# A hybrid RWKV-7 layer on one core: the scheduler's model of time exchanged

## The chip, the cores and the metric

The kernel runs on one core of a Trainium2 chip. The time is the device time of one execution in microseconds (us). The engines are named as in the profile: PE (TensorE, matrix products), DVE (VectorE), ACT (ScalarE), POOL (GpSimd) and SP (SyncE, which here issues most of the transfers). Each engine works through its own list of instructions in order, and an instruction waits at the head of the list until the semaphores it needs have been set by other engines or by transfers. What stands on which place of these lists is decided when the kernel is built.

## The reference

One step of one layer for 128 context tokens and 512 latent tokens, 2048 wide, all in fp32:

```
h = rmsnorm(x) * (1 + sc1) + sh1                 # sh1, sc1, ... from silu(c) @ w_mod
p = h @ w_in                                     # 2048 x 5408
o_a = rwkv7(shift(p[:, :3360]))                  # 16 heads of 64, forward and backward scan
o_b = gmlp(gelu(p[:, 3360:]))                    # 8 groups of 128, chunks of 128 tokens
x = x + g1 * (concat(o_a, o_b) @ w_out)
h = rmsnorm(x) * (1 + sc2) + sh2
x = x + g2 * ((silu(h @ w_gate) * (h @ w_up)) @ w_down)
y = final_rmsnorm(x);  also the final scan states
```

The scan of each head is S = S * w_t + (S a_t) b_t^T + v_t k_t^T, y_t = S r_t. The kernel works it in chunks of 64 tokens: inside a chunk with matrices, and from chunk to chunk with a recurrence.

## The kernel before

Every wide product is three matmuls: weights and activations are split into a high and a low part (`hi`, `lo`), and hi·hi, hi·lo and lo·hi are added up. A weight piece of 256 KB arrives in `raw`; `split` (L152) makes `hi` on ACT (L160) and `lo` on DVE (L161); there are three buffers of each. With two halves of 320 tokens, a piece is used in 24 matmuls of 128x320, called wide matmuls here.

The stages, in order of time:

1. The first stage (to about 135 us): transposes of x, the modulation columns of `w_mod` (`quarter`, loads `wt` L304, 1 MB each, five buffers), the norm, the first three column blocks of `w_in`, and 20 small loads of parameter rows (`rowA`, `rowB`, L265 to L278).
2. The mixer (to about 1190 us): 43 column blocks of `w_in`, 4128 wide matmuls (`win`, L182 to L184). Four pieces make one block in PSUM (`pb`, three buffers of a half each); `take` copies it with ACT into one of three `praw` buffers (L924) and hands it to a side step. Side steps are generators in three lists (mixA, mixS, mixM), run for a budget between the wide matmuls. For each pair of heads and each direction, `take_k` has PE products `pmm` (L491) and `pwa` (L568), then ACT (L548, L571, L584, L585) and DVE (L546 to L618) build `R` and `X`, PE makes `pG` (L629), DVE `GR` and `GA` (L637, L638), PE `pXT` and `pW` (L645, L654), and the result goes to `d_S` in DRAM. `solve` and `merge` invert the 64x64 chunk matrices (`psp`, `pblk`, `pM`). `mod_all` makes further modulation columns (`pm`, L872).
3. The recurrence (to about 1520 us): for each of 8 pairs 10 chunk records `rec` of 576 KB are loaded from `d_S`. `recur` makes `w_ps` (PE L1134), adds to it (DVE L1139), makes `u_ps` (PE L1149), copies it (DVE L1152, ACT L1153), makes `s_ps` (PE L1170) and the new state `SN` (DVE L1176), which the next `w_ps` needs. Latent and context chains run side by side, and pairs start OFF = 13 hops apart. Outputs are `y_ps` (L1100, L1105), then `pO` (L1217) and `pG` (L1235). Between them stand the wide matmuls of `wout_b` (L1002 to L1004, 768 of them), the half of the output projection that does not need the recurrence.
4. The rest of the output projection (L1392 to L1394) and the feed-forward part (L1539 to L1541), to the end.

The program text gives a first order and thereby a priority:

```
        if q == 0:
            halves = [pb.tile([P, HALF], F32, tag="big", name="big") for _ in range(2)]
        win(halves, q, *parts.pop(n), step=between)
        if q == 3:
            take(b, halves)
...
        mixA.finish(b - RAW)
        pr = bp.tile([P, T], F32, tag="praw", name="praw", bufs=RAW)
        for hf in range(2):
            S.copy(pr[:, HALF * hf:HALF * hf + HALF], halves[hf])
```

The order on the engines is then worked out by the scheduler of the tile framework. It goes through the program in a model of time of its own and puts next on an engine, of the instructions that the model says are ready, the one that stands first in the text. Two models can be chosen: a default one, which the kernel before uses, and one that plays the instructions on a timeline of the engines.

## Time and profile before

| | us |
|---|---|
| median of three runs | 3417.72 (3411.99 to 3417.9) |
| profiled execution, its own time | 3414.96 |
| its span | 3413.2 |
| PE busy in the span | 3189.6 (93%) |
| granted PE clock, mean | 0.975 |

A row by stage gives for each engine the busy time and in brackets the number of instructions recorded, then the granted PE clock as a share of full speed, the busy share of the transfer engines, and GB/s. A matmul's recorded time reaches from its issue to its modelled end, and matmuls overlap; the distance between starts tells what one costs. Rows of groups end with the idle time of the engine just before them and what ended it. Four instructions of a small 64-wide group appear as eight records.

### The profile page before, as it was taken

The page shows a single profiled execution, that of the slowest core. Times are in us where ns is not written, and L with a number is a line of the kernel's source. Part 1 is how long each engine was busy: PE and PEld are TensorE (multiplying, and loading weights), DVE is VectorE, ACT ScalarE, POOL GpSimd, SP SyncE. Part 2 cuts the span into 40 slices and gives each one's busy share as a digit, 9 for nine tenths or more (in the row PEclk, how much of TensorE's full clock was granted, in tenths as well). Part 3 has the DMA queues.
Part 4 walks back from the last instruction along what each step waited for, and adds up shares of the span by engine and source line. Part 5 has one row for each costly group of instructions (what it writes and reads, how often), then busy time and mean ns, then how long its engine had stood idle before and what let it go on. Part 6 is the DMA issues. An engine that isn't in the chain of part 4 may idle for free.

```text
span 3413.2 us, 72346 instructions
## 1 busy us (share of the span) xinstructions
PE 3189.6 (93%) x28100; PEld 2905.1 (85%) x28100; DVE 2512.9 (74%) x4357; ACT 1451.5 (43%) x3172; POOL 1251.9 (37%) x1090
## 2 busy tenths in 40 slices
PE   6899989889988899989999999999999999999996
PEld 3688768768766877778999999999999999999986
DVE  4548577676766656656888888888878877877787
ACT  3334444444443433324644444444444444443365
POOL 0001121122112112321056565565666645555543
PEclk8999999999999899989999999999999999999998
DMA  8766676676767577735533434334343354543453
GB/s 322 242 191 200 194 195 175 168 204 180 198 185 193 149 221 238 219 112 158 171 113 115 125 105 126 120 110 124 112 123 113 116 178 141 153 148 114 146 165 115
DMA packets 719137, 552.94 MB, mean 162 GB/s; under 512 B 99449, under 2 KB 652425, under 8 KB 709961
## 3 DMA queue, kind: packets, MB, share of 16 engines
q1 hardware_dynamic: 706472, 534.61, 52.4%
q0 software_dynamic: 9984, 13.13, 2.0%
q8 instruction: 221, 3.62, 0.4%
q14 instruction: 124, 1.01, 0.1%
q10 hardware_dynamic: 2336, 0.57, 0.1%
HBM read 438.77 MB, written 111.69 MB: 161 GB/s over the span
## 4 chain that ended last, share of the span: by engine, by line
PE 50%; DVE 6%; issue 5%; DMA 3%; POOL 1%; ACT 1%; DVEq 0%; SPq 0%; ACTq 0%; POOLq 0%
PE P L1541 13%; PE P L1539 13%; PE P L1540 13%; DVE lo L1358 2%; PE big L1002 2%; DMA d_os<-act 1%; PE big L1003 1%; PE big L1004 1%; PE u_ps L1149 1%; PE y_ps L1105 1%; PE s_ps L1170 1%; PE pO L1217 1%; DVE act L1660 1%; PE big L1394 1%; PE big L1392 1%
## 5 line engine op out<-in xcount | busy, mean ns | idle before, releaser
L1541 PE MATMUL P<-xo,lo 128*128 128x320 f32 x2352 | 731.6, 311 | 11.1 <-DVE lo L1358 11.1
L1539 PE MATMUL P<-xo,hi 128*128 128x320 f32 x2352 | 728.2, 310 | 2.0 <-ACT hi L1357 2.0
L1540 PE MATMUL P<-xo,hi 128*128 128x320 f32 x2352 | 727.6, 309 | 0.0
L1358 DVE TENSOR_TENSOR lo<-raw,hi 128x512 fp32r<-128x512 f32 x532 | 585.9, 1120 | 64.1 <-ACT hi L1357 60.0
L1357 ACT CAST hi<-raw 128x512 fp32r<-128x512 f32 x532 | 326.4, 621 | 415.2 <-PE P L1540 320.4
L182 PE MATMUL big<-h_hi,hi 128*128 128x320 f32 x1376 | 452.1, 329 | 10.2 <-ACT h_hi L344 3.7
L1541 PEld LDWEIGHTS P<-xo,lo 128*128 128x128 f32 x2352 | 442.4, 188 | 18.9 <-DVE lo L1358 18.8
L1539 PEld LDWEIGHTS P<-xo,hi 128*128 128x128 f32 x2352 | 442.6, 188 | 2.9 <-ACT hi L1357 2.7
L1540 PEld LDWEIGHTS P<-xo,hi 128*128 128x128 f32 x2352 | 442.4, 188 | 0.0
L184 PE MATMUL big<-h_hi,lo 128*128 128x320 f32 x1376 | 436.6, 318 | 5.6 <-DVE lo L161 5.5
L183 PE MATMUL big<-h_lo,hi 128*128 128x320 f32 x1376 | 437.5, 318 | 0.5 <-DVE h_lo L345 0.5
L1452 POOL TENSOR_TENSOR raw<-raw 128x512 f32<-128x512 f32 x252 | 408.0, 1628 | 11.6 <-DVE lo L1358 1.6
L1541 PE MATMUL P<-xd,lo 128*128 128x320 f32 x1232 | 385.1, 313 | 17.8 <-DVE lo L1358 17.5
L1539 PE MATMUL P<-xd,hi 128*128 128x320 f32 x1232 | 383.7, 311 | 9.9 <-ACT hi L1357 6.8
L1540 PE MATMUL P<-xd,hi 128*128 128x320 f32 x1232 | 381.9, 310 | 0.0
L182 PEld LDWEIGHTS big<-h_hi,hi 128*128 128x128 f32 x1376 | 265.1, 193 | 76.8 <-issue 44.5
L161 DVE TENSOR_TENSOR lo<-raw,hi 128x512 fp32r<-128x512 f32 x268 | 185.7, 696 | 182.0 <-ACT hi L160 179.9
L160 ACT CAST hi<-raw 128x512 fp32r<-128x512 f32 x268 | 165.0, 618 | 295.1 <-PE big L183 122.2
L184 PEld LDWEIGHTS big<-h_hi,lo 128*128 128x128 f32 x1376 | 265.6, 193 | 12.7 <-DVE lo L161 7.4
L183 PEld LDWEIGHTS big<-h_lo,hi 128*128 128x128 f32 x1376 | 265.9, 193 | 7.9 <-issue 3.7
L1357 ACT CAST hi<-rawd 128x512 fp32r<-128x512 f32 (+1 forms) x288 | 168.7, 587 | 240.3 <-PE P L1540 222.6
L1452 POOL TENSOR_TENSOR t<-raw 128x512 f32<-128x512 f32 x84 | 135.8, 1617 | 343.1 <-DMA raw<-in_w_ffn_up_dram 325.7
(372 smaller groups left out, 6404.3 us busy)
## 6 DMA issues: line engine op xcount, KB each, us to landing
wt<-in_w_mod_dram SPq DMA_DIRECT2D x96, 1024.0 KB
raw<-in_w_ffn_gate_dram SPq DMA_DIRECT2D x182, 256.0 KB
raw<-in_w_ffn_up_dram SPq DMA_DIRECT2D x182, 256.0 KB
rec<-d_S SPq DMA_DIRECT2D x80, 576.0 KB
raw<-in_w_in_dram SPq DMA_DIRECT2D x172, 256.0 KB
rawd<-in_w_ffn_down_dram SPq DMA_DIRECT2D x128, 256.0 KB
raw<-in_w_out_dram SPq DMA_DIRECT2D x96, 256.0 KB
xd<-d_os SPq DMA_DIRECT2D x66, 320.0 KB
```

Of the source, the lines that this page charges most:

```text
L160: S.copy(hi, raw)
L161: V.tensor_sub(lo, raw, hi.bitcast(F32))
L182: TE.matmul(halves[hf], hi[:, k, :], h_hi[:, kb, s], start=(kb == 0), stop=False)
L183: TE.matmul(halves[hf], hi[:, k, :], h_lo[:, kb, s], start=False, stop=False)
L184: TE.matmul(halves[hf], lo[:, k, :], h_hi[:, kb, s], start=False, stop=(kb == KB - 1))
L1002: TE.matmul(halves[hf], hi[:, k, :], o_hi[kb][:, s], start=(k == 0), stop=False)
L1357: S.copy(hi[:, 0:nk], raw[:, 0:nk])
L1358: V.tensor_sub(lo[:, 0:nk], raw[:, 0:nk], hi[:, 0:nk].bitcast(F32))
L1452: G.tensor_tensor(out=o[:, 0:nk], in0=p[:, 0:nk], in1=q[:, 0:nk], op=ALU.subtract)
L1539: TE.matmul(ps, hi[:, k, :], xk[:, 0, :], start=f, stop=False)
L1540: TE.matmul(ps, hi[:, k, :], xk[:, 1, :], start=False, stop=False)
L1541: TE.matmul(ps, lo[:, k, :], xk[:, 0, :], start=False, stop=l)
```

## The change

The scheduler works out the order with its timeline model in place of the default one. Nothing else is touched: the same instructions on each engine, the same tiles and buffers.

```
-    with _tile.TileContext(nc) as tc:
+    with _tile.TileContext(nc, schedule_with_timeline_sim=True) as tc:
```

The order moves on all engines from the start to the end of the recurrence; behind it only a few rows differ. Wide matmuls of the mixer are counted from 1 to 4128 below, so that places in the two orders can be compared.

On PE in the mixer, behind wide matmul 2304 of before, the last `pwa` of a direction of one pair reads:

```order
L568 MATMUL pwa<-waM,wh 128x320
L568 MATMUL pwa<-waM,wl 128x320
L872 MATMUL pm_6537<-wt,cT 2x512 x3
L182 MATMUL big<-h_hi,hi 128x320
L183 MATMUL big<-h_lo,hi 128x320
L184 MATMUL big<-h_hi,lo 128x320
```

From here 132 wide matmuls follow before the `pG` (L629) of that direction. In the new order, behind wide matmul 2436, the same `pwa` reads:

```order
L568 MATMUL pwa<-waM,wh 128x320
L568 MATMUL pwa<-waM,wl 128x320
L872 MATMUL pm_6537<-wt,cT 2x512 x12
L514 MATMUL pvt<-ident,zv 128x128 x3
L629 MATMUL pG<-R,X 128x128 x8
L514 MATMUL pvt<-ident,zv 128x128 x2
L182 MATMUL big<-h_hi,hi 128x320
```

The `pG` now stands behind its `pwa` with no wide matmul between; `pm` and `pvt` are side work of other lists. Over the 16 directions the distance from the last `pwa` to the first `pG` is 26 to 132 wide matmuls before, and 0 to 101 now, with 0 three times.

On PE late in the recurrence, in the hops of the last pairs, the order of before reads as follows (`w_ps`, `y_ps` and `s_ps` belong to the chains; `gh`, `g2h` and the like to the gate of a finished pair):

```order
L1235 MATMUL pG_18343<-gq,g2h 128x320
L1002 MATMUL big<-oh,hi 128x320
L1003 MATMUL big<-ol,hi 128x320
L1004 MATMUL big<-oh,lo 128x320
L1170 MATMUL s_ps<-rec 64x64 x4
L1002 MATMUL big<-oh,hi 128x320
L1235 MATMUL pG_18349<-gh,g2h 128x320
```

And the new one, behind the gate of a pair there:

```order
L1235 MATMUL pG_17160<-gq,g2h 128x320
L1170 MATMUL s_ps<-rec 64x64 x4
L1149 MATMUL u_ps<-W,rec 64x64 x4
L1100 MATMUL y_ps<-SN,rec 64x64 x2
L1105 MATMUL y_ps<-rec 64x64 x2
```

The wide matmuls of `wout_b` are gone from between the steps. Counted by `w_ps` groups, of which there are 288, the last of the 768 stands behind group 280 before and behind group 172 now.

On SP in the first stage the transfers before are

```order
L213 DMA xall<-in_x_sample_dram 128x2048 x2
L304 DMA wt<-in_w_mod_dram 128x4x512 x11
L159 DMA raw<-in_w_in_dram 128x4x128
L304 DMA wt<-in_w_mod_dram 128x4x512
L159 DMA raw<-in_w_in_dram 128x4x128
L304 DMA wt<-in_w_mod_dram 128x4x512 x3
L159 DMA raw<-in_w_in_dram 128x4x128
L304 DMA wt<-in_w_mod_dram 128x4x512
L265 DMA rowA<-in_mu_shift_dram 24x128
L267 DMA rowA<-in_mu_shift_dram 2x128
```

and now

```order
L213 DMA xall<-in_x_sample_dram 128x2048 x2
L304 DMA wt<-in_w_mod_dram 128x4x512 x5
L159 DMA raw<-in_w_in_dram 128x4x128 x3
L265 DMA rowA<-in_mu_shift_dram 24x128
L267 DMA rowA<-in_mu_shift_dram 2x128
L269 DMA rowA<-in_mu_shift_dram 1x32
```

The 20 small row loads, which end here with `rowB`, stand behind the fifth weight load `wt` now and behind the sixteenth before; the loads of `wt` from the sixth on follow them.

## The prediction

> **What bounds the kernel now.** I read the totals first, then the busy time by stage, then TensorE's (PE's) waits, then the durations in the stages whose order moves.
>
> ```profile
> span 3413.2 us, 72346 instructions
> PE 3189.6 (93%) x28100; PEld 2905.1 (85%) x28100; DVE 2512.9 (74%) x4357; ACT 1451.5 (43%) x3172; POOL 1251.9 (37%) x1090
> ```
> ```profile
> core 0: us, PE busy (x) PEld busy (x) DVE busy (x) ACT busy (x) POOL busy (x), PEclk, DMA share, GB/s
> 200.00:1200.00 1000.00, 905.33 (x10457) 761.34 (x10457) 696.39 (x1401) 433.40 (x929) 193.47 (x306) 0.97 0.68 186
> 1200.00:1500.00 300.00, 297.84 (x4438) 236.71 (x4436) 200.73 (x660) 106.35 (x488) 74.60 (x98) 1.00 0.72 212
> 1560.00:3300.00 1740.00, 1693.45 (x11316) 1670.38 (x11315) 1409.03 (x1886) 763.17 (x1430) 929.38 (x630) 0.99 0.44 132
> ```
>
> PE sets the time nearly everywhere, so a new order pays only by what PE waits less, or by what its own instructions cost less. The mixer (200 to 1200) holds 1000 - 905.33 = 94.7 us of PE idle time, the recurrence (1200 to 1500) 2.2 us. From the rest of the output projection on PE's order stays as it was but for a few rows, so the 1740 us of the third line carry no term. The waits of the mixer:
>
> ```profile
> engine line waited for: us in total, times, longest us
> PE pG L629 <- DVE X L618: 11.5, 10, 4.0
> PE pG L629 <- DVE GA L638: 10.8, 18, 1.9
> PE psp L740 <- DVE vt L727: 8.8, 4, 3.2
> PE pwa L568 <- DVE wl L533: 7.1, 2, 3.7
> ```
>
> They are many and small: a side step's matmul reaches PE's head a little before VectorE (DVE) or ScalarE (ACT) has its operand. That is what another order can remove, and what it can make worse.
>
> **The mixer.** I followed the dependences of both orders, with durations from the trace. Three things move.
>
> First, leads. In the new order side work mostly stands further behind its source: side matmuls with less than 24 wide matmuls (one weight piece, some 3.5 us) between source and use fall from 60 of 359 groups to 15 of 337. Of the 95 us, 6 lie in dense bursts; of the other 89 I take half away, -45. The ends: 0, if PE just meets other late work, and -80, if all but the 15 short leads' share is gone. Half is nearest to the list above: a wait names only the last of several late operands.
>
> Second, dense places. At six places of the new order (wide matmuls 1668, 1860, 2436, 2628, 3684 and 3780) a chain that runs PE, ACT, DVE, PE several times stands with no wide matmul in it. The next wide matmul needs its PSUM buffer copied to `praw` by ACT (L924), and that copy stands behind the chain on ACT. What such a chain costs, from its rows:
>
> ```profile
> L548 ACT ACT_TABLE_LOAD x8 | 10.3, 1283 | 0.1
> L548 ACT ACTIVATE ssq<-ssq 128x640 f32<-128x640 f32 x8 | 5.9, 740 | 6.0 <-DVE ssq L546 5.9
> L552 DVE RECIPROCAL ssq<-ssq 128x320 f32<-128x320 f32 x16 | 34.0, 2137 | 2.2 <-ACT ssq L548 2.2
> L581 DVE TENSOR_TENSOR_SCAN L<-scan,sg 128x320 f32<-128x320 bf16 x32 | 25.4, 825 | 0.2
> L614 DVE TENSOR_TENSOR X<-tha,L 64x640 f32<-64x640 f32 x16 | 12.9, 807 | 0.0
> L618 DVE TENSOR_TENSOR X<-fs,L 64x640 f32<-64x640 f32 x8 | 6.6, 821 | 0.1
> ```
>
> At 2436, `pmm` (L491) is followed by 1.28 + 0.74 us on ACT, two reciprocals (4.3 us), two scans (1.65), and on DVE nine more passes over 640 columns at about 0.81 (7.3) before `X` (L618) is there for `pG` (L629); with what else DVE's order puts between, 27.5 us from the last wide matmul to the next. PE has 9.1 us of work in it, so 18.4 us are idle. Done alike, the six give 7.5, 8.5, 9.7, 18.2, 18.4 and 26.3: 88.6 us, against 5.8 us in all such bursts of before: +83. Three of the chains also wait for a transfer, of which the trace has this time to landing:
>
> ```profile
> d_S<-TF POOLq DMA_DIRECT2D x16, 320.0 KB, 5.6
> ```
>
> I count 4 us for each such wait, an estimate, since part of the 5.6 lies under other steps; without any of it the six come to some 65 us, with 5.6 and some lateness of the queues to 110. I take the sum, as all its other steps are rows. Before shows the small form of the same wait, where `pG` stands only 26 wide matmuls behind `pwa`:
>
> ```profile
> 1064.81 2.08 PE L629 MATMUL pG<-R,X 64*128 64x128 f32 x16 [4.03 <-DVE X L618]
> ```
> ```profile
> 1064.00:1068.00 4.00, 3.19 (x24) 1.89 (x24) 3.69 (x6) 0.91 (x2) 0.00 (x0) 0.60 0.98 262
> ```
>
> 26 at 0.15 us are 4 us of cover, and 4 us of wait are left; with 0 in their place some 8 are left for this one piece of chain.
>
> Third, changes of the PE tile's shape. A small group between wide matmuls is dear:
>
> ```profile
> 1250.95 0.31 PE L1003 MATMUL big<-ol,hi 128*128 128x320 f32 x1
> 1251.10 0.31 PE L1004 MATMUL big<-oh,lo 128*128 128x320 f32 x1
> 1251.34 0.45 PE L1149 MATMUL u_ps<-W,rec 64*64 64x64 f32 x8
> 1251.72 0.42 PE L1002 MATMUL big<-oh,hi 128*128 128x320 f32 x1
> 1251.97 0.31 PE L1003 MATMUL big<-ol,hi 128*128 128x320 f32 x1
> ```
>
> Wide matmuls start 0.15 us apart, the small group 0.24 after the last of them, the next wide one 0.38 after that, its successor 0.25. Without a change I put the group at 0.23, so the pair of changes costs 0.09 + 0.15 + 0.10 = 0.34, 0.17 each. The Trainium skill (TensorEngine Tiling (Array Packing), Key Properties) says that changing the tiling mode drains TensorE; these rows agree, and it gives no figure. The mixer's changes go from 475 to 427: -8 us. Ends 0 and -8.
>
> The weight loads on SP and the steps of POOL move with the work that uses them. I cost both at nothing: three `raw` buffers hold two pieces ahead (7 us) at a transfer share of 0.68, and POOL is busy 193.47 of 1000 us. Should a load come late, its hi cast (L160) and the wide matmuls behind it wait, which the ends of the dense places take in.
>
> Mixer: -45 + 83 - 8 = +30.
>
> **The recurrence.** Its hops are chains of small matmuls and DVE additions, and the other half of the output projection (`wout_b`, 768 wide matmuls) stands between them as cover.
>
> ```profile
> L1139 DVE TENSOR_TENSOR W<-w_ps,rec 64x128 f32<-64x128 f32 x144 | 41.5, 288 | 17.7 <-PE w_ps L1134 13.5 <-PE swap L1074 0.3
> L1152 DVE COPY rec<-u_ps 64x128 f32<-64x128 f32 x79 | 22.2, 280 | 22.3 <-PE u_ps L1149 19.1 <-PE w_ps L1134 1.8
> L1176 DVE SCALAR_TENSOR_TENSOR SN<-s_ps,gend,SG 128x64 f32<-128x64 f32 x128 | 29.7, 278 | 23.3 <-PE s_ps L1170 22.6
> ```
>
> Before, the cover lasts to `w` group 280 of 288. In the new order it is used up at 172: the last 40% of the hops stand bare, and an early stretch too. A bare hop pays w, 0.29, u, 0.28, s, two times 0.28, with only the other chain's matmuls in between. Longest chain less PE work, over all stretches without cover: 5.3 us before, 36.7 after: +31. Its lower end is 20, if the handing over from engine to engine, which my sum counts at 0.04 to 0.08 us each, hides behind the other chain; its upper end is 50, if DVE, at 200.73 of 300 busy, is late with what stands ahead of these steps in its queue. I take the sum of rows. Shape changes fall from 536 to 432: 104 x 0.17 = -18, between -10 and -18. Recurrence: +13.
>
> **The first stage.** SP (the DMA queue's engine) issues 20 small row loads between the weight loads:
>
> ```profile
> 31.28 6.87 SPq L304 DMA_DIRECT2D wt<-in_w_mod_dram  x6
> 56.87 1.16 SPq L265 DMA_DIRECT2D rowA<-in_mu_shift_dram  x1
> 71.80 1.50 SPq L304 DMA_DIRECT2D wt<-in_w_mod_dram  x3
> ```
> ```profile
> 50.00:60.00 10.00, 8.44 (x38) 4.83 (x39) 5.42 (x12) 3.17 (x5) 0.00 (x0) 0.61 1.06 375
> 60.00:70.00 10.00, 10.00 (x76) 6.55 (x74) 1.22 (x4) 0.62 (x1) 0.00 (x0) 1.00 0.61 208
> 70.00:80.00 10.00, 4.99 (x32) 2.46 (x32) 7.44 (x19) 3.48 (x5) 0.00 (x0) 0.75 0.74 257
> ```
>
> While they are issued, 56.87 to 71.80, the transfer rate falls from 375 to 208 and 257 GB/s: 2.85 MB, or 7.6 us at 375, are not moved. In the new order they stand behind the first five `wt` and three `raw`, where SP waits for a free `wt` buffer until 31 us anyway. The cover is that wait; if it is too short (14.9 us of issuing), the sixth `wt` is late by a few us. -5, between -8 and +3.
>
> **The clock.** Long waits cost twice:
>
> ```profile
> L1217 PE MATMUL pO<-I,Y 64*64 64x64 f32 x40 | 4.9, 318 | 5.5 <-POOL Y L1209 4.8 <-DVE bv L1221 0.6
> L1217 PE MATMUL pO<-J,Y 64*64 64x64 f32 x40 | 4.6, 312 | 3.3 <-POOL Y L1209 3.3
> ```
> ```profile
> 1516.00:1520.00 4.00, 3.72 (x45) 3.60 (x46) 1.51 (x3) 0.00 (x0) 0.00 (x0) 0.50 0.00 0
> 1520.00:1524.00 4.00, 2.72 (x9) 1.92 (x8) 1.09 (x2) 0.00 (x0) 0.00 (x0) 0.50 0.00 0
> 1524.00:1528.00 4.00, 4.00 (x16) 4.00 (x16) 0.41 (x1) 0.62 (x1) 0.00 (x0) 0.50 0.47 153
> ```
>
> After 8 us of waits, 12 us ran at half clock: up to 6 us lost; after the 4.03 us at 1064.81 the clock was 0.60 over 4 us, 1.6 us lost. The six long stretches so lose 10 to 36. Against that stand the mixer's 0.97, or 30 us off the full clock, which shrink with the small waits. I take +20 - 15 = +5, ends -15 and +30. The Trainium skill (TensorE: Matmul & The Clock Gate, Part 1) puts the array at half rate after an idle window of about 3.4 us until a busy one has passed; the pieces above agree, and by it alone six stretches would cost six times 1.7, an estimate of 10 us.
>
> **The sum.** -5 + 30 + 13 + 5 = +43 on the profiled execution's 3414.96 us (span 3413.2): 3458. That execution lies 2.8 us under the median, inside the runs' 3411.99 to 3417.9. A measurement tells 0.2%, 7 us, from no change.
>
> **Rivals.**
> - *The leads win (faster).* One mechanism, in the mixer: with DVE and ACT further ahead nearly all of the 89 us go (-79 in place of -45), and with these waits the half-clock pieces (-15 in place of +5). That is 54 us less than my sum: 3404. The list of small waits speaks for it; against it, a dense place starts every queue anew, and each of its steps is a measured duration. It ends under 3408 once waits and clock together give 50 us more than I put. Chance 0.15.
> - *The bare hops are slow (much slower).* The last stretch has 68 us of PE work in small groups and 30 us of idle time; if the clock falls there as it did after 1516, these groups take 318 in place of 228 ns, 1.39 times: +27, and with the upper ends of the chains (+19) and of the clock in the mixer (+10) 3514. No row of before shows the clock under such short gaps. Chance 0.22.
> - *The order does not matter.* If engines take up what they missed within a few steps, gains and losses cancel, within 7 us of 3415. The 26-matmul row speaks against it. Chance 0.05.
> - *My sum*, 3425 to 3490: 0.58.
>
> The range 3395 to 3520 leaves out under 2 in 10. Faster 0.16, same 0.05, slower 0.79; the two tails of my own case go to their neighbours.
>
> **What would show it.** Right: six PE waits of 7 to 26 us in the mixer, named by DVE `X`, ACT `praw` or `pG`; the sum of the other waits about halved; PE under 85% busy in the last 100 us of the recurrence, with waits on L1139, L1152 and L1176; GB/s without the dip at 60 to 80. Wrong: wide matmuls running on at those six places because ACT's copy comes early, or PE's idle time in the recurrence still near 2 us.

## The result and the profile after

| | before | changed |
|---|---|---|
| median of the runs | 3414.85 (3405.62 to 3417.9) | 3493.94 (3484.51 to 3500.46) |
| profiled execution, its span | 3413.2 | 3498.7 |
| granted PE clock, mean | 0.975 | 0.947 |

The changed kernel takes 1.0234 times as long (95% interval 1.0202 to 1.0266): 79 us more between the medians, 85.5 between the two profiled executions, of which the changed one is the slowest of its four. What follows is told against the profiled pair.

The head of the page of the changed kernel:

```profile
span 3498.7 us, 72391 instructions
PE 3209.6 (92%) x28100; PEld 2939.7 (84%) x28100; DVE 2502.0 (72%) x4357; ACT 1454.0 (42%) x3172; POOL 1264.5 (36%) x1090
```

Busy time does not tell it: PE has 20 us more, in 85 us more of span. The stages do. I cut both executions at the same events: the last `pm` of the first stage, the last wide matmul of the mixer, the first of `wout_b`, the last `w_ps`, the first and the last matmul of the feed-forward part. The mixer and the recurrence between such cuts, first before, then changed (stretch; its length; busy time of PE, weight loads, DVE, ACT, POOL; granted clock; transfer share; GB/s):

```profile
127.20:1163.30 1036.10, 943.71 (x10639) 793.07 (x10638) 710.01 (x1450) 448.40 (x957) 193.38 (x307) 0.97 0.67 184
1170.50:1499.10 328.60, 323.50 (x4605) 260.90 (x4605) 222.21 (x701) 118.32 (x512) 76.78 (x100) 0.99 0.72 215
```
```profile
123.50:1211.60 1088.10, 952.42 (x10518) 808.70 (x10518) 717.83 (x1445) 446.48 (x956) 198.73 (x304) 0.91 0.64 175
1213.80:1580.20 366.40, 339.74 (x4696) 289.04 (x4698) 231.31 (x717) 122.11 (x518) 80.30 (x102) 0.90 0.63 193
```

| stage | before | changed | difference | PE idle before, changed | at half clock before, changed |
|---|---|---|---|---|---|
| first stage | 127.2 | 123.5 | -3.7 | | 34.1, 30.7 |
| mixer | 1036.1 | 1088.1 | +52.0 | 92.4, 135.7 | 58.0, 198.0 |
| to the first of `wout_b` | 7.2 | 2.2 | -5.0 | | |
| recurrence | 328.6 | 366.4 | +37.8 | 5.1, 26.7 | 6.9, 71.7 |
| rest of the output projection, second norm | 227.9 | 237.8 | +9.9 | | 30.7, 37.5 |
| feed-forward part | 1659.3 | 1651.7 | -7.6 | | 13.7, 6.8 |
| tail | 26.9 | 29.0 | +2.1 | | |

So the mixer and the recurrence carry the loss, and both lose in two ways: PE idles 43 and 22 us longer, and it runs 140 and 65 us longer at half clock. PE's waits in the mixer, longest sums first:

```profile
engine line waited for: us in total, times, longest us
PE pm L872 <- DMA wt<-in_w_mod_dram: 37.2, 15, 5.2
PE pW L654 <- ACT XT L647: 21.2, 7, 6.2
PE pG L629 <- DVE X L615: 19.2, 5, 11.9
PE pG L629 <- DVE GA L638: 9.9, 8, 2.7
```

Before, the longest sum was 11.5 us and the longest wait 4.3. Now fewer waits are longer, and the first of them is `pm` for its weights, which the prediction put at nothing: its three transfers were those through `d_S`. The six dense places are where PE's long gaps lie. Their stretches from the last wide matmul to the next:

```profile
435.60:469.60 34.00, 17.09 (x91) 6.43 (x90) 21.91 (x44) 12.42 (x26) 0.74 (x1) 0.65 0.66 209
509.10:535.20 26.10, 15.98 (x280) 9.44 (x278) 20.62 (x41) 10.06 (x24) 4.33 (x9) 0.71 0.70 218
679.50:707.70 28.20, 14.45 (x70) 5.47 (x69) 23.73 (x49) 10.49 (x21) 1.23 (x1) 0.62 0.58 183
750.60:776.30 25.70, 18.23 (x317) 11.42 (x315) 19.54 (x41) 10.84 (x25) 5.61 (x9) 0.66 0.55 163
1045.90:1061.90 16.00, 7.10 (x33) 2.90 (x32) 12.65 (x24) 7.37 (x14) 3.80 (x1) 0.70 0.52 183
1085.30:1131.90 46.60, 23.53 (x363) 17.94 (x362) 26.21 (x52) 17.46 (x41) 16.48 (x28) 0.57 0.41 98
```

Length less PE busy gives 16.9, 10.1, 13.8, 7.5, 8.9 and 23.1: 80.2 us idle in 176.6 us, at a clock of 0.57 to 0.71. By name, 33.2 us of them are waits of `pm` for its weights, 17.5 waits of `pG` for `X`, 9.1 of `pwa` for `sg`; the rest is spread. In the last place, the longest, there is no wait of `pm`, and `pG` waits 11.9 us for `X`.

In the recurrence `wout_b` ends at 1471.5, and the last `w_ps` stands at 1580.2. Of that bare stretch:

```profile
1472.00:1500.00 28.00, 24.20 (x506) 20.10 (x507) 19.48 (x71) 10.20 (x56) 7.55 (x13) 0.93 0.82 254
1500.00:1540.00 40.00, 32.13 (x584) 26.02 (x582) 24.28 (x81) 12.99 (x64) 14.15 (x17) 0.76 0.72 218
1540.00:1560.00 20.00, 20.00 (x298) 16.84 (x298) 9.16 (x34) 5.33 (x36) 0.00 (x0) 0.50 0.43 129
1560.00:1580.00 20.00, 16.09 (x255) 13.25 (x254) 10.79 (x33) 6.35 (x28) 10.58 (x14) 0.81 0.20 61
```

But for one of 3.8 us for `oh` (L1392, at 1535) the waits in it are at most 1.3 us, and from 1540 to 1560 there is none at all: PE is busy for all of the 20 us, at half clock. The clock falls to half at 1496.1, for 10.2 us, at 1526.8, for 34.1, and once more at 1567.8, for 6.8. The 3.4 us just before the first two falls are

```profile
1492.70:1496.11 3.41, 1.74 (x44) 1.37 (x44) 1.46 (x5) 2.37 (x11) 3.01 (x7) 1.00 0.95 314
1523.42:1526.83 3.41, 1.81 (x42) 1.48 (x42) 2.21 (x8) 2.29 (x9) 3.24 (x6) 1.00 0.86 240
```

In both PE is busy for only half of the time, by many gaps of which none is longer than 1.3 us.

### The profile page after: what moved, and what is told of

Same layout as the page of the kernel before. It is cut to its first block, busy times and chain, and to the rows that moved or that the text cites. A ratio compares the mean times of both kernels' runs of the same rounds, so it can differ in the third digit from the quotient of the medians.

```text
span 3498.7 us, 72391 instructions
## 1 busy us (share of the span) xinstructions
PE 3209.6 (92%) x28100; PEld 2939.7 (84%) x28100; DVE 2502.0 (72%) x4357; ACT 1454.0 (42%) x3172; POOL 1264.5 (36%) x1090
## 4 chain that ended last, share of the span: by engine, by line
PE 52%; DVE 10%; DMA 7%; issue 4%; ACT 2%; POOL 1%; SPq 0%; DVEq 0%; ACTq 0%; POOLq 0%
PE P L1541 12%; PE P L1539 12%; PE P L1540 12%; DVE lo L1358 3%; DMA d_os<-act 2%; PE big L182 1%; PE big L184 1%; PE big L183 1%; PE big L1392 1%; PE big L1002 1%; PE big L1393 1%; PE big L1394 1%; DVE act L1660 1%; PE big L1004 1%; PE big L1003 1%
## 5 line engine op out<-in xcount | busy, mean ns | idle before, releaser
L182 PE MATMUL big<-h_hi,hi 128*128 128x320 f32 x1376 | 444.5, 323 | 5.1 <-ACT h_hi L344 3.2
```

The source lines that it names most:

```text
L182: TE.matmul(halves[hf], hi[:, k, :], h_hi[:, kb, s], start=(kb == 0), stop=False)
```

## The experiments

The instructions have the same names whichever model orders them. So a kernel can be built twice: once with the default model, to read the order, and then with the timeline model, with the order of chosen instructions pinned. A pin is an edge that fixes the order on one engine and adds no wait:

```
def _pin(tc, want, skip=()):
...
    info = mybir.DependencyInfo(mybir.DependencyClass.NoSync, mybir.DependencyReason.DATA)
    by = {i.name: i for i in tc.nc.cur_bb.bb.instructions}
    for names in want.values():
        for a, b in zip(names, names[1:]):
            tc.add_manual_dep(by[b], a, info, reason="pin")
...
    _, order = build(False)
    nc, order = build(True, order)
```

`_wanted(k, engine)` says which instructions are pinned; k is the place in the program text, `MARK["mix"]` the start of the mixer's code, `MARK["rec"]` that of the recurrence, `MARK["out"]` that of the part behind it. `want` holds one list for each engine. The edits below start from `return True`, which pins everything. Each run is compared with before on its own chip.

**One stage alone.** First the new order up to the end of the mixer, then the new order in the recurrence.

```
-        return True
+        return k >= MARK["rec"]
```

> The new order from the start to the end of the mixer, the order of before from the recurrence on (pinned on every engine). Theory A (the loss comes from two places that add up: mixer with its six dense places, recurrence without cover): the mixer's +48 us to its last wide matmul stay, the recurrence is as before, so 3415 + 45 = 3460 (3450 to 3470), with some 135 us of PE idle time and some 200 us at half clock up to the last wide matmul. Theory B (what is lost later is a follow-up of the mixer's delays, by the clock and by buffers that come late): the recurrence is slow again although its order is the old one, 3480 or more.

```
-        return True
+        return k < MARK["rec"] or k >= MARK["out"]
```

> The order of before up to the end of the mixer, the new one in the recurrence. Theory A: the recurrence loses what it lost in the changed kernel, 38 us from the first wide matmul of the output projection to the last w, so 3415 + 40 = 3455 (3445 to 3465); no cover behind w group 172 or so, and more than 50 us at half clock in the last 110 us of it. Theory B: 3425 or less.

The first took 3471.83 us, 1.0161 of before (1.0136 to 1.0186); the second 3439.91, 1.0069 (1.0043 to 1.0096). The two excesses add up to 2.30%, beside 2.34% for the whole change, so there are two places that add up, as theory A says. But the shares are not those I gave, 45 and 40 us; they are some 54 and 22, and both times lie outside theory A's ranges, the first by 2 us and the second by 5. The recurrences of the two runs, in this order:

```profile
1218.30:1559.20 340.90, 326.30 (x4657) 263.51 (x4653) 229.07 (x713) 120.42 (x514) 77.82 (x102) 0.98 0.69 207
```
```profile
1168.90:1517.80 348.90, 323.08 (x4618) 274.42 (x4622) 224.94 (x707) 116.81 (x506) 80.18 (x100) 0.94 0.66 202
```

A new order in the recurrence alone costs it 348.9 - 328.6 = 20 us, not 38. It is not the changed kernel's order place by place, since the model makes it anew behind the old mixer, but it has the same feature: `wout_b` ends behind `w_ps` group 176, where the changed kernel has 172, and 98 us of hops stand bare, where that has 109. PE idles as long, 25.8 beside 26.7 us; at half clock it runs for 44.4 beside 71.7. And behind the new mixer the old order costs 12 us more than before, so part of theory B holds as well. Most of those 12 is one wait:

```profile
PE pxT L1260 <- DMA x1T<-in_x_prompt_dram: 7.7, 1, 7.7
```

A load that the mixer's order leaves late on its queue is waited for at the start of the recurrence.

**The first stage alone.**

```
-        return True
+        return k >= MARK["mix"]
```

> Only the first stage in the new order, all behind it as before. The 20 small row loads stand where SP waits for a weight buffer anyway: 3 to 4 us less, 3411, with no dip of the GB/s at 60 to 80 us. Rival: the loads of the first stage are bound by the transfers in sum, and the place of the small ones is all one: 3415 within 2.

3409.26 us, 0.9983 of before (0.9964 to 1.0002). The interval just reaches 1, so the run settles nothing between the two expectations. The transfers ran without the dip:

```profile
60.00:70.00 10.00, 10.00 (x60) 7.36 (x56) 1.35 (x3) 1.21 (x2) 0.00 (x0) 0.76 1.05 386
70.00:80.00 10.00, 10.00 (x76) 6.29 (x72) 1.61 (x6) 1.82 (x3) 0.00 (x0) 1.00 1.06 378
```

But the last `pm` of the first stage stood at 126.9 us, hardly sooner than the 127.2 of before. Of the ten executions of this study with the new order in this stage, the changed kernel among them, six have it at 123.3 to 123.8 and four at 126.9 to 127.1; four more with the old order have it at 125.1 to 128.2. The four late ones share a pattern: at half clock they have 6.8 us from 58 us on, 3.4 from 89 and 3.4 from 113, where the changed kernel has 3.4 from 59 and 3.4 from 83. So the transfers lose their dip as was forecast, and in some executions the time saved is gone again, and these have more half clock. That the half clock takes it back is not shown.

**Half of the engines.** In the mixer PE in the order of before and the others free, and the reverse.

```
-        return True
+        return k >= MARK["rec"] or k >= MARK["mix"] and "PE" in str(engine)
```

> PE in the order of before from the mixer on, and all engines in the order of before from the recurrence on; in the mixer DVE, ACT, POOL and SP in the order the timeline model gives beside that. Theory A (it is PE's place for the side matmuls that makes the dense places and the small waits): PE's idle time in the mixer is near that of before, 92 us, and the time 3415 within 10. Theory B (the orders of DVE and ACT carry it, the copies to praw above all): 3440 or more, or 3400 or less if their order is what shortens the small waits.

```
-        return True
+        return k >= MARK["rec"] or k >= MARK["mix"] and "PE" not in str(engine)
```

> The counterpart of the run with PE's old order: in the mixer DVE, ACT, POOL and SP in the order of before, PE as the timeline model orders it beside them; from the recurrence on all as before. Theory A (orders fit as a set; either half alone loses): 3440 to 3480. Theory B (the order of DVE is the bad part, PE's follows it): 3415 within 10, with PE idle time in the mixer under 105 us.

Both lose far more than the whole new order of the mixer did (1.0161): 3502.99 us (1.0255, 1.0219 to 1.029) and 3531.28 (1.0348, 1.0317 to 1.038). The idle time of PE in the mixer is 1122.3 - 968.9 = 153 and 1144.0 - 974.9 = 169 us, beside 92 before and 136 changed. PE's waits in the mixer, of the first kernel and of the second:

```profile
PE pG L629 <- DVE X L615: 26.6, 8, 5.9
PE pvt L514 <- DVE zv L454: 26.1, 4, 10.9
PE pG L629 <- DVE GA L638: 14.6, 14, 3.0
```
```profile
PE pm L872 <- DMA wt<-in_w_mod_dram: 60.0, 23, 6.3
PE big L182 <- ACT hi L160: 18.8, 16, 4.9
PE big L184 <- DVE lo L161: 17.4, 15, 2.5
```

With PE as before, the other engines' free order brings `X` and `zv` late; with the others as before, PE's free order waits for weights and for the hi and lo casts. My theory A of the first run (PE's order decides) fell, and the time is in the range of theory B (3440 or more). In the second run theory B (DVE's order is the bad part) fell, and theory A (either half alone loses) holds, with a loss far above the one I gave. That an order is good only for the other engines' orders is the reading I prefer, but it is not shown: the free engines did not get the changed kernel's order, the model made a third one beside the pins. These runs also fit a model that orders badly whatever it is left to order.

**What sets the length of a dense place.** The wait that is named most there is `pm` for `wt`, and 61 `pm` matmuls, four for each weight load, stand in these places. So I kept `pm` at its old place among the wide matmuls: `KEPT` holds the `pm` and the first and third matmul of `win`, and only these are pinned.

```
-                    TE.matmul(pm[32 * j:32 * j + 2, :], ...)
+                    KEPT.add(TE.matmul(pm[32 * j:32 * j + 2, :], ...).ins.name)
...
-                    if n in at and _wanted(at[n], e):
+                    if n in at and n in KEPT:
```

> The changed kernel (3494 us) with one thing held back: the pm matmuls (L872) and the wide matmuls stand to each other on PE as before, so that the dense places hold at most 4 pm matmuls each; everything else is scheduled with the timeline model. Theory A (the chain through ACT and DVE sets how long a dense place lasts, and the waits of pm for their weights lie beside it): 3485 to 3505, more than 115 us of PE idle time in the mixer. Theory B (pm waits for its 1 MB weight load, for which there is one buffer in the mixer, and this sets the length of the places): the 37 us of such waits go, with some clock: 3440 to 3470, idle time in the mixer under 105.

3543.27 us, 1.0387 (1.0357 to 1.0417): slower than the changed kernel by 49 us, with 1140.8 - 968.3 = 172 us of idle time.

```profile
PE pvt L514 <- DVE zv L454: 31.9, 4, 12.0
PE pG L629 <- DVE X L615: 28.5, 4, 11.0
PE pW L654 <- ACT XT L647: 25.3, 12, 5.5
PE pm L872 <- DMA wt<-in_w_mod_dram: 19.2, 10, 4.1
```

The waits of `pm` halve and those for `zv`, `X` and `XT` grow by more. Theory B fell: taking the waiting `pm` away shortens nothing, and the dependent chain shows itself in its place. The time is above theory A's range, too. That the chain alone sets the length is not shown by this, since the rest of the order moved too.

**Another buffer for the blocks.** The dense places seem to lie where the wide matmuls have run ahead by all three `praw` buffers: with a fourth, they move on by one block in the order. It needs 2.5 KB, which I took from XT and GR; the control has these with one buffer, too, and three `praw`.

```
-                    GR = bk.tile([P, 4, CH], F32, tag="GR", name="GR", bufs=2)
+                    GR = bk.tile([P, 4, CH], F32, tag="GR", name="GR", bufs=1)
...
-                XT = bz.tile([P, 4, P], F32, tag="XT", name="XT", bufs=2)
+                XT = bz.tile([P, 4, P], F32, tag="XT", name="XT", bufs=1)
```

> Control for the next run: the timeline model with one buffer each for XT and GR (L636, L646, and the weights of L527 that share GR), in place of two, which frees 3 KB per partition. Five dense places in the order, most of them where the changed kernel has them (1668, 1860, 2436, 3684, 3780). Both theories: somewhat slower than the changed kernel, 3495 to 3530, for waits on the writes of XT and GR.

```
-RAW = 3
+RAW = 4
```

> As the control, with the room given to a fourth praw buffer (RAW = 4). The dense places move by one block of 96 wide matmuls (1860 to 1956, 3684 to 3780, 3780 to 3876). Theory A (a dense place is where the wide matmuls have used up the praw buffers and must wait for a side chain; one buffer more gives one block more before that): the places move but do not end, and only those are lighter that another buffer carries to the next chain: 10 to 40 us under the control. Theory B (praw has nothing to do with it): within 8 us of the control.

> The same buffers (RAW = 4, one XT, one GR) with the default model. If the mixer is limited by praw in the default order too, 10 to 20 us under before: 3395 to 3405; if the one buffer for XT and GR costs more than praw gives: 3420 to 3440.

The control took 3593.84 us (1.0528, 1.0502 to 1.0555), with a fourth buffer 3623.58 (1.0599, 1.0581 to 1.0618), and the default model with a fourth buffer 3490.02 (1.0218, 1.02 to 1.0236). All three expectations missed. The mixer, and the rest up to the last `w_ps`, of the control and of the kernel with four buffers (the second stretch starts here at the last wide matmul of the mixer):

```profile
127.10:1326.40 1199.30, 980.74 (x10518) 826.93 (x10518) 717.01 (x1444) 447.66 (x955) 198.88 (x306) 0.87 0.57 159
1326.40:1688.40 362.00, 335.42 (x4822) 285.04 (x4822) 234.27 (x722) 124.11 (x522) 82.48 (x103) 0.92 0.64 196
```
```profile
127.00:1315.30 1188.30, 970.52 (x10158) 819.45 (x10158) 710.29 (x1428) 441.99 (x944) 195.31 (x303) 0.87 0.58 159
1315.30:1698.10 382.80, 344.99 (x5180) 294.10 (x5182) 240.26 (x738) 128.59 (x534) 82.13 (x105) 0.90 0.62 190
```

PE's idle time in the mixer is 218.6 and 217.8 us: a fourth `praw` buffer takes none of it away. It lets 360 more of PE's matmuls slip behind the last wide one, and the recurrence pays for them. So the number of `praw` buffers says where a dense place lies in the order, and not what it costs. The second buffer of XT and GR, which nobody had in view, is worth some 100 us under the timeline model. It is not this model's alone: with one buffer of each, and the fourth `praw` buffer, the default model loses 74 us against before.

**The clock in the bare stretch.** In the changed kernel's own order I put 8 idle products ahead of each group of `y_ps` of the last three pairs, into columns of PSUM that nobody reads; the tile of `y_ps` is made wider for them.

```
...
+                for _ in range(FILL if p >= 5 else 0):
+                    FILLS.add(TE.matmul(yf[0][:, 128:384], gh[:, 0:P], gh[:, 0:256], start=True, stop=True).ins.name)
```

> The changed kernel in its own order (3494 us), with 8 idle products of 128x256 into unused columns of PSUM ahead of each group of y matmuls of the last three pairs: 192 matmuls, some 23 us of PE work whose result nobody reads. Theory A (in the bare stretch the clock falls because PE is not busy enough, and that costs more than the idle time): half clock in the recurrence falls from 66 us to under 35, and the time is 3475 to 3495 in spite of the added work. Theory B (the bare hops are bound by the chain alone, the clock adds little): the work fills some of the 22 us of idle time and the rest comes on top, 3500 to 3517.

3508.2 us, 1.0285 (1.0253 to 1.0316). The recurrence:

```profile
1217.50:1592.70 375.20, 358.18 (x4871) 305.93 (x4874) 231.64 (x717) 122.17 (x517) 81.42 (x103) 0.94 0.62 189
```

Its time at half clock fell from 71.7 us (the 66 of the expectation takes the clock's record 11 us too late) to 44.4, its idle time from 26.7 to 17.0, and it took 9 us longer for 23 us of products and their 48 changes of tile shape (5 to 8 us at the prices below). The clock's part shows in the time of a matmul of the same kind from 1472 to 1595, first in the changed kernel, then with the filling:

```profile
L1149 PE MATMUL u_ps<-W,rec 64*64 64x64 f32 x240 | 19.3, 267 | 3.2 <-DVE W L1139 2.9
```
```profile
L1152 PE MATMUL u_ps<-W,rec 64*64 64x64 f32 x248 | 16.5, 234 | 0.2
```

234 ns is near the 227 of before, and nearly all of the wait is gone. So that the clock falls for want of work on PE holds; that it costs more than such filling does not. The time is in theory B's range (3500 to 3517), and theory A's is missed. But B's ground, that the clock adds little, does not fit the 27 us of half clock that went, and A's mark of under 35 us was not reached either.

**The price of a change of tile shape.** The kernel before with its default model, but `wout_b` gives way after 12 wide matmuls.

```
-                yield 0.4
+                if k % 4 == 3:
+                    yield 0.4 * 4
```

> The kernel before with its default schedule, but wout_b gives way after 12 wide matmuls in place of 3, which lowers the changes of tile shape in the recurrence by some 180. At 0.17 us each (the price both traces give) that is -31 us: 3385. Rival: groups of 1.8 us are more than a hop needs and leave others bare, waits on L1139, L1152 and L1176 come up and eat half or all of it: 3400 to 3425.

3409.71 us, 0.9992 (0.9975 to 1.001): no difference that can be told. In the recurrence there is one:

```profile
1177.80:1496.20 318.40, 313.44 (x4617) 265.41 (x4618) 218.54 (x701) 119.21 (x513) 78.38 (x100) 0.99 0.73 221
```

It is 328.6 - 318.4 = 10.2 us shorter, all of it PE busy time, and no wait came up. So the time lies in the rival's range, but not by the rival's waits. The mixer, in the same order as before, took 6.8 us longer in this execution, with 20 us more at half clock. I had miscounted the changes: those between wide and small fall from 403 to 237, but groups of 64*64 and 128*64 now meet each other, and these rise from 126 to 203. The sum falls by 89, not by 180: 10.2 / 89 = 0.11 us each. Fitting the distances between starts in the recurrences of before, of the changed kernel and of this one, where PE has no gap and the full clock, with a price per recorded matmul and one per change, gives an estimate of 0.08 to 0.12 us for each common kind of change. That is below the 0.17 of the prediction.

**What helped, together.** The new order in the first stage, the old one behind it, and `wout_b` by 12.

> What helped a little, together: the new order in the first stage alone, the order of the default model behind it, and wout_b in groups of 12 wide matmuls. The first stage without the dip of the transfers (3 us), the recurrence 10 us shorter by 90 changes of tile shape less: 3402, between 3395 and 3410. If neither was real: 3414 within 5.

3404.74 us, 0.9965 (0.9951 to 0.9978), as expected. The gain over before, 0.35%, is small, but its interval leaves out 1. Both steps it was made of show in the trace: the last `pm` at 123.8, the recurrence 319.0 us. How much of it is the first stage's, with its two levels, is left open.

```profile
1169.50:1488.50 319.00, 314.19 (x4617) 266.42 (x4618) 218.98 (x701) 119.36 (x513) 78.36 (x100) 0.98 0.72 221
```

## Why the prediction was right, and where it was not

The forecast was 3458 and slower; the time is 3494, within the range, at nearly twice the loss. By its steps:

- *The dense places, +83.* Right in place and size: all six are there, with 80 us of idle time against 88.6 forecast (at 2436, the one worked out step by step, 13.8 against 18.4). The step's account of them is only half confirmed, and so the match of the sums is in part luck. In five of the six the largest sum of waits is that of `pm`, 33 of the 80 us; `pm` has one weight buffer in the mixer, and I had counted these `pm` as work alone and the weight loads at nothing. The 12 us for three transfers through `d_S` did not come: no wait in the six places is named by one. Nor is any named by the copy to `praw`, and of the six waits of 7 to 26 us that I gave as the sign there is one, of 11.9; the others are sums of shorter waits. In the run that keeps `pm` apart, waits on the chain through DVE and ACT grow by more than those of `pm` shrink. (The lower end that the prediction gives for this sum, 65, does not follow: without three times 4 us it is 76.6.)
- *Leads, -45.* Idle time outside the dense places went from 92.4 - 5.8 = 86.6 to 135.7 - 80.2 = 55.5: -31. Mis-sized by a third.
- *Changes of shape, -8 and -18.* By the trace, changes in the recurrence fell from 530 to 427, as counted; at 0.11 to 0.17 that is -11 to -17, and the 0.11 measured above makes the lower end the likelier.
- *The bare hops, +31.* Idle time in the recurrence rose by 21.6, with 15.6 us of it in the bare stretch; part of the rest belongs to the late load that the mixer leaves behind. Mis-sized, at the lower end of its range of 20 to 50.
- *The clock, +5.* This is the term that failed. PE's busy time in the mixer rose by 8.7 although the changes of shape should have taken 8 from it, and in the recurrence by 16.2 in place of a fall by 11 to 17. If nothing else changed PE's busy time, that puts the clock at some 17 and 27 to 33 us. Of the second, an estimated 5 is work, since 91 more recorded matmuls lie in the recurrence now; that leaves 39 to 45 in all, in place of 5. The prediction had set off the gains of the small waits against the losses of the long ones, and had kept the clock in the bare hops for a rival, since no row of before showed it there. It also read the price of a long wait too low: behind the waits for `Y` before, the clock is at half from 1508.5 to 1529.0, 20.5 us, and not for 12.
- *First stage, -5.* Measured -3.7 in the changed kernel; four other executions of the same order show next to nothing.
- *Everything behind, 0.* The stages behind the recurrence and the step before it give -5.0 + 9.9 - 7.6 + 2.1 = -0.6. They cancel; I did not look for the cause of each.

Of the rivals, the leads did not win. The mechanism of the bare hops came true, in the clock and in matmuls of 324 ns in place of 227 from 1540 to 1560:

```profile
L1149 PE MATMUL u_ps<-W,rec 64*64 64x64 f32 x46 | 4.7, 324 | 0.0
```

Its price did not: its terms make the recurrence 13 + 27 + 19 = 59 us longer, and it is 37.8 longer. The Trainium skill (TensorE: Matmul & The Clock Gate, HAM oscillation) gives the rule that gaps above some 3.4 us on PE cost the clock. At four of the dense places the trace agrees: their longest waits are 3.65 to 11.9 us, at a clock of 0.57 to 0.71. At the other two (2628 and 3684) the clock is 0.66 and 0.70 with no wait above 3.2 us. In the bare stretch, too, the rule does not suffice: half clock sets in at 1496, after 25 us in which the longest wait was 1.30 us. What the first two falls there have in common is the half-empty 3.4 us just before them.

Open: what sets the length of a dense place, and why the timeline model puts such places into the order. No trace shows what a model thinks is ready, and the fourth buffer did not remove them.

## What to carry to other kernels

When a scheduler's model is exchanged, look in the new order for stretches in which a chain over several engines stands with no independent matmul in it, and for the point at which the covering work is used up; the durations of the old trace priced the six places together within 9 us here, and the bare hops within 10, though many of the waits had other names. Add the clock to the price of every such stretch, not only of long waits. And measure before you mix orders: pinning one engine to a good order beside others that are free cost more here than either whole order did.

## What the hardware showed that I had not expected

PE can be recorded as busy without a gap and yet run at half clock: 20 of 20 us, inside 34 us at half clock, with 64-wide matmuls nearly alone; why the clock did not come back sooner is open. It can fall to half with no wait above 1.3 us, when PE is busy for 1.74 of the 3.41 us before. And 192 matmuls that computed nothing wanted took 27 us of half clock away. The same order of the mixer took 1036.1, 1036.7, 1038.8, 1039.9 and 1042.9 us in five executions, with 58 to 79 us at half clock, so a gain of 5 us in one stage does not show in the time of a single run.
